# One decoder layer for a prompt and a sample group: second half of the layer with channels on the partitions

## The chip, the cores and the metric

The kernel runs on one core of one Trainium2 chip, in 4-byte floats. The metric is the device time of one execution in microseconds (us). A core has TensorE (PE, matrix products into PSUM), VectorE (DVE), ScalarE (ACT), GpSimd (POOL), and SyncE (SP), whose queue starts the DMAs here.

## The reference, cut to what matters

One layer serves a prompt of 2048 tokens and 8 sample tokens; the width is 1024, the feed-forward's 4096.

```
mix = concatenate([o_r, o_m]) @ w_out                 # o_r, o_m: the two mixers' outputs
h  = layer_norm(ALPHA * x + mix, ln1_g, ln1_b)        # mean and variance over the 1024 channels
ff = square(relu(h @ w_ff1)) @ w_ff2
y  = layer_norm(ALPHA * h + ff, ln2_g, ln2_b)
```

The first half of the layer (input projection, an RWKV-7 and a Mamba-2 mixer, and the states) is the same before and after, and so is what the two norms compute.

## The kernel before

The prompt is cut into 4 blocks of 512 tokens. The sample's 8 tokens ride along with block 1 (`smp` in the code). First comes the input projection of all blocks; the mixers of block 0 run beside it. Then `tail(b)` computes output projection, first norm, feed-forward and second norm of each block, and the mixers of block b+1 are recorded in between, at a set rate. The order of the instructions on each engine is made when the program is built, from the order of recording, priorities and buffers; each engine then works its own queue in that order.

Every large product is done in three parts (`mm3`, L163 to L168): an operand is split into a high and a low part (`split`, L196: ACT makes the high one, DVE or POOL the difference), and high x high, high x low and low x high add up in PSUM. Weights come in pieces of 128 x 512 (`wpiece`, L202).

In `tail` a matrix of tokens by channels is built, with the tokens on the partitions: four tiles `hs` of 128 tokens x 1024 channels. The output projection (L1287 to L1330) goes by halves of 256 tokens: for each quarter of the channels and each tile, 24 products of 256 columns, whose sum is added to ALPHA x (L1308). Bank statistics (`stats`, L1203), a square root by Newton steps (`rsqrt`, L175) on one or two columns and one ACT step per tile (L1221) give the normalised rows. For the feed-forward channels are wanted on the partitions: TensorE transposes 128 x 128 pieces (`tr`, L1340) and ACT applies gain and bias on the way out of PSUM (L1346), then the split follows. The first FIRST = 4 tiles of the feed-forward are done for the first 256 tokens while the second half is still being normalised (L1351), then for the second half (L1363). Gain and bias of the rows themselves, needed for ALPHA h, follow beside the feed-forward (`gain`, L1224). `ff1` (L1440) makes 128 of the 4096 channels for the block, with channels on the partitions. The second matrix (L1392 to L1426) goes by 8 steps g of 4 such tiles: hidden values stationary, 512 channels of the weights moving, 12 products of 512 columns for each of 8 outputs. The sample's 8 hidden columns are split into 16 (`hids`) and have 8 narrow products of 512 columns of their own in each half of a step (L1398 to L1401); its output projection has 16 of 256 columns for each quarter (L1318). `fold16` adds the two parts.

The second norm of block b is recorded during the output projection of block b+1 (`late`, L1314); in the last block it goes tile by tile behind each tile's last addition (`norm`, L1232).

PSUM has three banks of tag b and one of tag a for these products, used in turn (`bank`, L1274).

Of the kernel before, what the change touches and what calls it, by code (L numbers as in the profile page):

```python
# [13 lines left out]
ALU = mybir.AluOpType  # L14
# [9 lines left out]
POOLN = (True, True, False, False)  # L24
# [5 lines left out]
        ("xf", 1), ("uv", 2), ("bt", 1), ("st", 2), ("r1", 1), ("hids", 8))  # L30
# [26 lines left out]
for _name, _w in (  # L57
    ("mu", 14), ("w0", 4), ("a0", 4), ("kk", 4), ("ka", 4), ("rk", 4), ("lnw", 4), ("lnb", 4),
    ("cw", 32), ("cb", 8), ("gn", 4), ("ds", 4), ("g1", 8), ("b1", 8),
# [10 lines left out]
for _name, _w in (  # L70
    ("ident", 128), ("scm", 128), ("m1", 64), ("m2", 64), ("bm", 4), ("d16", 16), ("tri", 128),
    ("b64", 128), ("cen", 128), ("s16", 8), ("sel", 2), ("one", 2),
):
    CCOL[_name] = (_n, _w)
    _n += _w
# [3 lines left out]
def shape_constants():  # L79
# [25 lines left out]
    put("one", 1.0)  # L105
    return c


class K:
# [30 lines left out]
    def wide(self):  # L140
        return self.sb("g4", (128, 2, 520)).rearrange("p a t -> p (a t)")[:, :1024]

# [32 lines left out]
    def rsqrt(self, x, n, p=128):  # L175

        nc = self.nc
        y = self.sm(f"rsy{n}", [128, n])[:p]
        t = self.sm(f"rst{n}", [128, n])[:p]
# [4 lines left out]
        if n == 1:  # L184
            nc.vector.tensor_scalar(out=x, in0=x, scalar1=-0.5, scalar2=None, op0=ALU.mult)
        for _ in range(3):
            if n == 1:
                nc.vector.scalar_tensor_tensor(out=t, in0=y, scalar=x, in1=y, op0=ALU.mult, op1=ALU.mult)
                nc.vector.scalar_tensor_tensor(out=y, in0=t, scalar=1.5, in1=y, op0=ALU.add, op1=ALU.mult)
            else:  # L190
                nc.vector.scalar_tensor_tensor(out=t, in0=y, scalar=-0.5, in1=y, op0=ALU.mult, op1=ALU.mult)
                nc.vector.tensor_mul(t, t, x)
                nc.vector.scalar_tensor_tensor(out=y, in0=t, scalar=1.5, in1=y, op0=ALU.add, op1=ALU.mult)
# [39 lines left out]
    def setup_mix(self):  # L233
# [79 lines left out]
        self.osT = self.mp.tile([128, 8, 16], F32R, name="osT")  # L313
# [25 lines left out]
    def load_o(self, b, half):  # L339
        return self.load_act(lambda k: self.s_o[b][:, k, :], range(4 * half, 4 * half + 4))  # L340
# [594 lines left out]
    def sample(self):  # L935
# [162 lines left out]
        os_ = t(8, 8)  # L1098
# [86 lines left out]
        self.split(os_, self.osT[:, :, 0:8], self.osT[:, :, 8:16])  # L1185
# [17 lines left out]
    def stats(self, h, bs, q):  # L1203
        self.nc.vector.bn_stats(bs[:, q, :], h[:, q * 512:(q + 1) * 512])

    def ln(self, tiles, bs, p):

        nc = self.nc
        n = len(tiles)
        mv = self.sm("mv", [128, 4, 2])[:p, :n]  # L1210
        for i in range(n):
# [417 lines left out]
```

## Time and profile before

| | |
|---|---|
| median of 3 runs | 2891.64 us (2886.47 to 2894.46) |
| profiled execution | 2881.87 us |
| its span | 2880.1 us |
| mean granted TensorE clock | 0.982 of full speed |
| PE, DVE, ACT, POOL busy | 97%, 69%, 45%, 13% |

The profile is of one execution. Busy times are shares of the span from the first to the last instruction. Two TensorE products are in flight at a time, so the duration of one is longer than the distance from one start to the next; that distance is the rate. A 4-byte product that is not split (weights and data as plain floats) stands in the trace as two instructions.

### The profile page before, as it was taken

To read this page: it belongs to the slowest core of one execution; us is meant where nothing else is said; L and a number is where in the kernel's file an instruction comes from. 1 tells how busy PE (TensorE), PEld (TensorE's weight loads), DVE (VectorE), ACT (ScalarE), POOL (GpSimd) and SP (SyncE) were. 2 spreads that over 40 slices of the span, in tenths; PEclk is the share of its full clock that TensorE was granted. 3 is DMA by queue.
4 is the path that set the end of the run, shared out by engine and by line. 5 is a ranking of instruction groups with operands and counts; after the bars stand their busy time and mean duration, and the time that the engine had idled before them with its cause. 6 is when DMAs were issued, how large, how long until landed. Compare 5 with 4: busy or idle time off the path is not lost.

```text
span 2880.1 us, 52319 instructions
## 1 busy us (share of the span) xinstructions
PE 2786.3 (97%) x19114; PEld 2310.9 (80%) x19114; DVE 1979.4 (69%) x4841; ACT 1285.9 (45%) x2493; POOL 364.5 (13%) x508
## 2 busy tenths in 40 slices
PE   9999999999989999998899999998999999899997
PEld 7798987777878777787788888887777778888886
DVE  7878878878777767676866666568766656754446
ACT  5554644554536333434544444336343334543332
POOL 2322212222321000002200000022000001200001
PEclk9999999999989999998999999999999999899999
DMA  6655655555744434346434344254443335433232
GB/s 207 191 169 150 185 152 165 156 176 160 211 138 133 131 110 130 110 125 215 136 93 120 115 116 121 85 196 131 120 138 114 109 103 167 158 103 95 88 103 70
DMA packets 333766, 395.54 MB, mean 137 GB/s; under 512 B 84990, under 2 KB 191060, under 8 KB 333500
## 3 DMA queue, kind: packets, MB, share of 16 engines
q1 hardware_dynamic: 333508, 392.20, 45.4%
q8 instruction: 150, 2.46, 0.4%
q14 instruction: 108, 0.88, 0.1%
HBM read 331.32 MB, written 60.81 MB: 136 GB/s over the span
## 4 chain that ended last, share of the span: by engine, by line
PE 79%; DVE 10%; DMA 4%; issue 4%; ACT 2%; SPq 1%; POOL 0%; DVEq 0%; POOLq 0%; ACTq 0%
PE psb L166 18%; PE psb L167 18%; PE psb L168 17%; PE psm L152 7%; PE psa L166 4%; PE psa L168 4%; PE psa L167 4%; PE psc L152 2%; PE psa L152 2%; PE psb L152 1%; DVE w L200 1%; PE psm L173 1%; PE psy L741 1%; DVE lr L655 1%; DVE rX L656 1%
## 5 line engine op out<-in xcount | busy, mean ns | idle before, releaser
L199 ACT ACTIVATE w<-wr 128x512 fp32r<-128x512 f32 (+1 forms) x836 | 518.8, 627 | 604.5 <-PE psb L168 237.2
L200 DVE TENSOR_TENSOR w<-wr,w 128x512 fp32r<-128x512 f32 x712 | 510.8, 722 | 230.3 <-ACT w L199 226.5
L166 PE MATMUL psb<-act,w 128*128 128x512 f32 (+2 forms) x1768 | 628.4, 356 | 6.3 <-ACT act L199 5.5
L167 PE MATMUL psb<-act,w 128*128 128x512 f32 (+2 forms) x1768 | 621.1, 352 | 0.6 <-DVE act L200 0.6
L168 PE MATMUL psb<-act,w 128*128 128x512 f32 (+2 forms) x1768 | 616.9, 349 | 0.0
L166 PEld LDWEIGHTS psb<-act,w 128*128 128x128 f32 x1768 | 335.9, 190 | 55.5 <-ACT act L199 6.0
L168 PEld LDWEIGHTS psb<-act,w 128*128 128x128 f32 x1768 | 336.3, 190 | 45.6 <-DVE w L200 0.2
L167 PEld LDWEIGHTS psb<-act,w 128*128 128x128 f32 x1768 | 337.0, 191 | 44.7 <-DVE act L200 2.6
L166 PE MATMUL psb<-w,g 128*128 128x512 f32 x788 | 317.0, 404 | 9.5 <-ACT w L199 9.5
L167 PE MATMUL psb<-w,g 128*128 128x512 f32 x788 | 314.6, 399 | 0.0
L168 PE MATMUL psb<-w,g 128*128 128x512 f32 x788 | 312.5, 397 | 0.0
L200 POOL TENSOR_TENSOR w<-wr,w 128x512 fp32r<-128x512 f32 x124 | 180.2, 1458 | 717.5 <-ACT w L199 703.6
L1504 DVE TENSOR_TENSOR g<-psb,g 128x512 f32<-128x512 f32 x173 | 118.8, 687 | 163.2 <-PE psb L168 162.6
L166 PEld LDWEIGHTS psb<-w,g 128*128 128x128 f32 x788 | 148.6, 189 | 46.1 <-ACT w L199 10.3
L168 PEld LDWEIGHTS psb<-w,g 128*128 128x128 f32 x788 | 148.4, 188 | 33.6 <-DVE g L200 0.2
L167 PEld LDWEIGHTS psb<-w,g 128*128 128x128 f32 x788 | 149.0, 189 | 32.5 <-DVE w L200 0.2
L200 DVE TENSOR_TENSOR g<-r,g 128x256 fp32r<-128x256 f32 (+1 forms) x172 | 97.1, 565 | 82.5 <-ACT g L199 81.6
L1454 ACT ACTIVATE r<-psb 128x512 f32<-128x512 f32 (+2 forms) x130 | 63.2, 487 | 190.2 <-PE psb L168 188.3
L166 PE MATMUL psa<-act,w 128*128 128x256 f32 (+2 forms) x336 | 116.4, 346 | 0.0
L167 PE MATMUL psa<-act,w 128*128 128x256 f32 (+2 forms) x336 | 114.6, 341 | 0.0
L168 PE MATMUL psa<-act,w 128*128 128x256 f32 (+2 forms) x336 | 114.1, 340 | 0.0
L655 DVE TENSOR_TENSOR lr<-rX,lr 128x4 f32<-128x4 f32 (+14 forms) x480 | 100.7, 210 | 10.8
(389 smaller groups left out, 5207.3 us busy)
## 6 DMA issues: line engine op xcount, KB each, us to landing
wr<-in_w_ff_dram SPq DMA_DIRECT2D x512, 256.0 KB
wr<-in_w_in_dram SPq DMA_DIRECT2D x208, 256.0 KB
wr<-in_w_out_dram SPq DMA_DIRECT2D x112, 256.0 KB
lr<-d_l SPq DMA_DIRECT2D x256, 64.0 KB
s_m<-g SPq DMA_DIRECT2D x48, 256.0 KB
ms<-s_m SPq DMA_DIRECT2D x16, 768.0 KB
wr<-in_xT_dram SPq DMA_DIRECT2D x32, 256.0 KB
s_ar<-g SPq DMA_DIRECT2D x16, 512.0 KB
```

Of the source, the lines that this page charges most:

```text
L152: return self.nc.tensor.matmul(out, l, r, start=start, stop=stop)
L166: nc.tensor.matmul(out, l[0], r[0], start=first, stop=False)
L167: nc.tensor.matmul(out, l[0], r[1], start=False, stop=False)
L168: nc.tensor.matmul(out, l[1], r[0], start=False, stop=last)
L173: self.nc.tensor.transpose(out, in_, self.cst[p0:p0 + k, o + p0:o + p0 + k])
L199: nc.scalar.activation(hi, raw, AF.Copy)
L200: (eng or nc.vector).tensor_tensor(out=lo, in0=raw, in1=hi.bitcast(F32), op=ALU.subtract)
L655: nc.vector.tensor_tensor(out=row, in0=X[:, :, s + 1:16], in1=row, op=ALU.mult)
L656: nc.vector.tensor_reduce(X[:, :, s:s + 1], lr[:, :, 17 * s:16 * s + 16], axis=AX.X, op=ALU.add)
L741: acc = lambda o, l, r, start, stop: nc.tensor.matmul(o, l, r, start=start, stop=stop, skip_group_check=True)
L1454: nc.scalar.activation(rl, ps, AF.Relu)
L1504: self.nc.vector.tensor_tensor(out=h, in0=ps, in1=h, op=ALU.add)
```

## The change

Everything in `tail` now has the channels on the partitions: `hs` are four tiles of 128 x 2 x 520, two groups of 128 channels each, with 512 tokens and the sample's 8 behind them. The weights become the stationary operand of output projection and second matrix, the activations the moving one. ALPHA x is loaded from the transposed input, and the result is stored transposed; the host turns it round. The sample's tokens are 8 more columns of the second half (264 in place of 256); for that the second matrix goes by halves in block 1, and also in the last step of the last block, where the first half's norm is recorded between the second half's products.

A norm is now done for 256 (or 264) tokens at a time, over channels on the partitions. Means come from TensorE: eight products with a column of ones, each giving 32 equal rows, in four column groups of the array, so that four partial sums stand on 4 x 32 partitions; ACT copies them to SBUF, and one 128 x 128 product with a constant adds them and gives every partition the mean. The same is done with the squares. `rsqrt` works on the full 128 x 256. There are no transposes, no bank statistics, no `fold16`, and no gain and bias over rows; gain and bias are ACT's scale and bias again.

The core of the diff:

```diff
+    def chan_mean(self, src, m, held):
+        p = self.bank()
+        one = self.con("one")[:, 0:1].to_broadcast([128, 32])
+        self.row([(p[32 * (k % 4):32 * (k % 4) + 32, :m], one, src(k), k < 4, k >= 4) for k in range(KT)], held)
+        part = self.sb("r", (128, 512))[:, :m]
+        self.nc.scalar.activation(part, p[:, :m], AF.Copy)
+        p = self.bank()[:, :m]
+        self.mm(p, self.con("mean").to_broadcast([128, 128]), part)
+        return p
+
+    def norm(self, hs, o, m, gain, bias, put, held):
         nc = self.nc
+        seg = [h[:, :, o:o + m] for h in hs]
+        wide = lambda a: a.unsqueeze(1).to_broadcast([128, 2, m])
+        mean = self.chan_mean(lambda k: seg[k // 2][:, k % 2, :], m, held[o])
+        yield
+        sqs = []
+        for h in seg:
+            nc.vector.tensor_tensor(out=h, in0=h, in1=wide(mean), op=ALU.subtract)
+            sqs.append(self.sb("sq", (128, 2, 264))[:, :, :m])
+            sq = nc.scalar.activation(sqs[-1], h, AF.Square)
+        yield
+        var = self.chan_mean(lambda k: sqs[k // 2][:, k % 2, :], m, sq)
+        ln = self.sb("ln", (128, 3, 264))
+        x, y, t = (ln[:, i, :m] for i in range(3))
+        nc.vector.tensor_scalar(out=x, in0=var, scalar1=LN_EPS, scalar2=None, op0=ALU.add)
+        rs = self.rsqrt(x, m, yt=(y, t))
+        yield
+        for q, h in enumerate(seg):
+            nc.vector.tensor_tensor(out=h, in0=h, in1=wide(rs), op=ALU.mult)
+            for a in range(2):
+                k = 2 * q + a
+                nc.scalar.activation(h[:, a], h[:, a], AF.Identity, scale=self.par(gain, k), bias=self.par(bias, k))
+            put(q)
             yield
...
+        for half, (o, m) in enumerate(cols):
+            for i in range(KT):
+                k = i if half == 0 else KT - 1 - i
+                if half == 0 or i:
+                    wo = [self.wpiece(A["w_out"][k, :, h * 512:(h + 1) * 512], (4, 128)) for h in range(2)]
...
+                ps = self.bank()[:, :m]
+                for c in range(KT):
+                    l = [wo[c // 4][s][:, c % 4, :] for s in range(2)]
+                    r = [act[c][:, s, o:o + m] for s in range(2)]
+                    self.mm3(ps, l, r, c == 0, c == KT - 1)
+                held[o] = self.accum(hs[k // 2][:, k % 2, o:o + m], ps, True)
+                next(ln, 0)
+                next(self.late, 0)
+                yield 2.6
             for _ in ln:
                 pass
+            ln = self.norm(hs, o, m, "g1", "b1", split_hT(o, m), held)
...
+        norms = [self.norm(hs, o, m, "g2", "b2", store(o, m), held) for o, m in cols]
...
+            end = last and nxt is None
+            for o, m, k in [(o, m, k) for o, m in cols for k in range(KT)] if end else \
+                    [(o, m, k) for k in range(KT) for o, m in segs]:
...
+                ps = self.bank()[:, :m]
                 for f in range(4):
-                    l = [hid[f][0][:, s, i * 128:(i + 1) * 128] for s in range(2)]
-                    r = [w2[f][s][:, 0, :] for s in range(2)]
+                    l = [w2[k // 4][f][s][:, 0, c] for s in range(2)]
+                    r = [hid[f][0][:, s, o:o + m] for s in range(2)]
                     self.mm3(ps, l, r, f == 0, f == 3)
+                held[o] = self.accum(hs[k // 2][:, k % 2, o:o + m], ps, g == 0)
...
+                if end and o:
+                    next(norms[0], 0)
...
+        self.late = itertools.chain(*norms)
```

How the queues change is shown at three places. The first is VectorE's queue in the move from block 2 to block 3, from the last addition of the output projection on. `psb_28160` is the PSUM bank of the last output projection group, `g_...` are tiles of `hs`, `w_` weight pieces being split, `obs` and `omv` statistics, `act_` the operands of the feed-forward. Before:

```order
L1308 SCALAR_TENSOR_TENSOR g_4513_27859<-g_4513_27859,psb_28160 128x256
L200 TENSOR_TENSOR w_28404<-wr_28402,w_28404 128x512
L1204 BN_STATS obs_27446<-g_4513_27859 128x6
L1212 BN_AGGR omv_28298<-obs_27446 128x2
L200 TENSOR_TENSOR act_28193<-r_28197,act_28193 128x256
L200 TENSOR_TENSOR act_28201<-r_28205,act_28201 128x256
```

Now, where `psb_28885` holds the mean of the second norm of block 2 (`g_3496`, `g_3511`), `act_28819` to `act_28871` belong to the first half of block 3, and `ln_` are the square root's tiles; `psb_28897` is the last output projection group:

```order
L1403 SCALAR_TENSOR_TENSOR g_4408_28088<-g_4408_28088,psb_28897 128x256
L1214 TENSOR_TENSOR g_3496_22606<-g_3496_22606,psb_28885 128x2x256
L190 TENSOR_TENSOR act_28819<-g_4442_28312,act_28819 128x256
L190 TENSOR_TENSOR act_28822<-g_4442_28312,act_28822 128x256
L1214 TENSOR_TENSOR g_3511_22736<-g_3511_22736,psb_28885 128x2x256
L190 TENSOR_TENSOR act_28868<-g_4455_28414,act_28868 128x256
L190 TENSOR_TENSOR act_28871<-g_4455_28414,act_28871 128x256
L190 TENSOR_TENSOR w_29153<-wr_29151,w_29153 128x512
L1221 TENSOR_SCALAR ln_28948<-psb_28946 128x256
```

Behind the last addition there now stands the rest of the norm of the block before, and then, from the 21st instruction on, the block's own second half; the first operand of that half is the 48th instruction behind the addition.

The second place is TensorE's queue at the same point. Before, transposes (L173) follow the last output projection group, and `psb_28194`, `psb_28202` are their banks:

```order
L168 MATMUL psb_28160<-w_28127,act_27392 128x256
L173 MATMUL psb_28194<-cst,g_4462_27467 128x128
L173 MATMUL psb_28194<-cst,g_4463_27469 128x128
L173 MATMUL psb_28202<-cst,g_4462_27467 128x128
L173 MATMUL psb_28202<-cst,g_4463_27469 128x128
```

Now the sums of squares (`sq_`) of the block before follow, then the spreading product (`r_28944` is the copy of its partial sums), and the feed-forward (`psb_28988`):

```order
L165 MATMUL psb_28897<-act_28027,w_28894 128x256
L149 MATMUL psa_28935<-sq_28924,cst 32x256 x2
L149 MATMUL psa_28935<-sq_28927,cst 32x256 x2
L149 MATMUL psa_28935<-sq_28930,cst 32x256 x2
L149 MATMUL psa_28935<-sq_28933,cst 32x256 x2
L149 MATMUL psb_28946<-r_28944,cst 128x256
L163 MATMUL psb_28988<-act_28721,w_28979 128x256
```

No transpose is left, and the sums stand in the queue ahead of products that do not need them.

The third place is the end of TensorE's queue. Before, it ends with the last product of the second matrix:

```order
L166 MATMUL psb_31087<-w_30917,g_5000_30812 128x512
L167 MATMUL psb_31087<-w_30917,g_5000_30812 128x512
L168 MATMUL psb_31087<-w_30917,g_5000_30812 128x512
L1620 UNCONDITIONAL_BRANCH
```

Now mean and variance of the second half of the last block follow it (`g_4408` to `g_4455` are the four tiles, `sq_` their squares):

```order
L165 MATMUL psb_31890<-g_4947_31521,w_31666 128x256
L149 MATMUL psb_31904<-g_4408_28088,cst 32x256 x2
L149 MATMUL psb_31904<-g_4421_28190,cst 32x256 x2
L149 MATMUL psb_31904<-g_4442_28312,cst 32x256 x2
L149 MATMUL psb_31904<-g_4455_28414,cst 32x256 x2
L149 MATMUL psb_31915<-r_31913,cst 128x256
L149 MATMUL psa_31929<-sq_31918,cst 32x256 x2
L149 MATMUL psa_31929<-sq_31921,cst 32x256 x2
L149 MATMUL psa_31929<-sq_31924,cst 32x256 x2
L149 MATMUL psa_31929<-sq_31927,cst 32x256 x2
L149 MATMUL psb_31940<-r_31938,cst 128x256
```

Eighteen 4-byte products, eight for each sum and one to spread it, now stand behind the last large product, where none stood.

## Rows read from the trace of the kernel before

**Rows 1.** The page, part 1: busy us (share of the span) and instructions.
```profile
PE 2786.3 (97%) x19114; PEld 2310.9 (80%) x19114; DVE 1979.4 (69%) x4841; ACT 1285.9 (45%) x2493; POOL 364.5 (13%) x508
```

**Rows 2.** Windows: stretch, us, busy of PE, PEld, DVE, ACT, POOL; clock, DMA, GB/s.
```profile
820.00:900.00 80.00, 69.97 (x662) 62.96 (x661) 55.51 (x146) 45.58 (x102) 17.41 (x16) 0.86 0.51 156
1390.00:1450.00 60.00, 50.44 (x396) 41.13 (x394) 45.55 (x127) 33.12 (x75) 10.36 (x10) 0.83 0.42 129
1950.00:1990.00 40.00, 31.59 (x218) 26.62 (x217) 35.72 (x70) 23.31 (x40) 12.81 (x8) 0.87 0.51 165
2480.00:2530.00 50.00, 40.58 (x286) 37.72 (x285) 34.48 (x61) 31.48 (x71) 9.38 (x6) 0.83 0.37 126
2600.00:2800.00 200.00, 200.00 (x864) 161.87 (x862) 86.15 (x128) 74.03 (x124) 0.00 (x0) 1.00 0.31 96
```

**Rows 3.** Waits of TensorE: who waited for whom, us in total, times, longest.
```profile
PE psb L173 <- DVE g L1308: 9.9, 4, 4.7
PE psa L173 <- DVE g L1308: 5.0, 2, 2.9
PE psb L173 <- ACT r L1346: 2.5, 3, 1.3
```

**Rows 4.** Timeline of TensorE in block 1's second matrix: start, duration, operation.
```profile
1914.63 1.32 PE L152 MATMUL psa<-w,hids 128*16 128x512 f32 x5
1915.79 0.39 PE L166 MATMUL psb<-w,g 128*128 128x512 f32 x1
...
1918.58 0.28 PE L166 MATMUL psb<-w,act 128*128 128x256 f32 x1
...
1921.40 0.39 PE L166 MATMUL psb<-w,g 128*128 128x512 f32 x1
```

**Rows 5.** Groups of instructions by shape, TensorE: count, busy us, mean ns, idle before.
```profile
L173 PE MATMUL psb<-cst,g 128*128 128x128 f32 x96 | 22.0, 332 | 12.8 <-DVE g L1308 9.9 <-ACT r L1346 2.5 <-ACT r L1454 0.4
L152 PE MATMUL psb<-w,hids 128*16 128x512 f32 x80 | 21.0, 399 | 0.0
L152 PE MATMUL psb<-w,osT 128*16 128x256 f32 x48 | 6.0, 277 | 0.0
```

**Rows 6.** Timeline of TensorE: mixer products of 64 and of 128 outputs.
```profile
908.48 0.45 PE L152 MATMUL psm<-m,m 128*64 128x128 f32 x4
...
910.43 0.50 PE L166 MATMUL psb<-act,w 128*128 128x512 f32 x1
...
913.79 1.02 PE L152 MATMUL psm<-m,m 128*128 128x256 f32 x4
914.46 0.58 PE L168 MATMUL psb<-act,w 128*128 128x512 f32 x1
```

**Rows 7.** Groups of instructions by shape, VectorE.
```profile
L1504 DVE TENSOR_TENSOR g<-psb,g 128x512 f32<-128x512 f32 x173 | 118.8, 687 | 163.2 <-PE psb L168 162.6
L1226 DVE TENSOR_TENSOR g<-g,g 128x1024 f32<-128x1024 f32 x28 | 36.5, 1310 | 3.9 <-ACT g L1221 2.9 <-PE psb L173 1.0
L1204 DVE BATCH_NORM_STATS2 fbs<-g 128x6 f32<-128x512 f32 x32 | 22.0, 690 | 0.6
L749 DVE TENSOR_TENSOR st<-psc,st 128x256 f32<-128x256 f32 x32 | 13.5, 423 | 19.0 <-PE psc L152 18.7
L582 DVE TENSOR_SCALAR g<-g 128x512 f32<-128x512 f32 x16 | 9.2, 573 | 3.9 <-ACT g L571 3.6
```

**Rows 8.** Timeline of TensorE behind the waits of the last stretch.
```profile
2500.03 0.41 PE L166 MATMUL psb<-act,w 128*128 128x256 f32 x1
...
2500.67 0.42 PE L166 MATMUL psb<-act,w 128*128 128x256 f32 x1
```

**Rows 9.** Groups of instructions by shape, ScalarE.
```profile
L1346 ACT ACTIVATE r<-psb,prm 128x256 f32<-128x256 f32 x42 | 22.6, 559 | 13.9 <-PE psb L173 11.2 <-DVE act L200 2.4
```

**Rows 10.** Timeline: the last large product and the last step of VectorE.
```profile
2864.98 0.40 PE L168 MATMUL psb<-w,g 128*128 128x512 f32 x1
...
2875.23 1.41 DVE L1247 SCALAR_TENSOR_TENSOR g<-g,frsy,g 128x512 f32<-128x512 f32 x2
```

More of the change, by code (lines that the diff above doesn't have):

```diff
@@ L71 @@
     ("ident", 128), ("scm", 128), ("m1", 64), ("m2", 64), ("bm", 4), ("d16", 16), ("tri", 128),
[L72 removed]
+    ("b64", 128), ("cen", 128), ("s16", 8), ("sel", 2), ("one", 2), ("mean", 1),
 ):
@@ L105, in shape_constants @@
     put("one", 1.0)
+    put("mean", 1.0 / (32 * D))
     return c
@@ L339, in load_o @@
     def load_o(self, b, half):
-        return self.load_act(lambda k: self.s_o[b][:, k, :], range(4 * half, 4 * half + 4))
+        return self.load_act(lambda k: self.s_o[b][:, k, :], range(4 * half, 4 * half + 4),
+                             sample=self.osT if b == self.sblk else None)
     def wpieces(self, j, halves=(0, 1)):
@@ L1357, in tail @@
+        first = []
+        for f in range(FIRST):
+            first.append(self.ff1(f, hT, cols[:1]))
+            next(ln, 0)
+            yield 2.6
+        for _ in ln:
+            pass
         self.pf = "f"
-        g1 = self.affine(1)
-        gain = itertools.chain(*([self.gain(h, 128, *g1) for h in hs[:4]] +
-                                 ([self.gain(hs[4][0:8], 8, *g1)] if smp else [])))
-        segs = [(0, 256), (256, 264)] if smp else [(0, 512)]
+        segs = cols if smp else [(0, TB)]
@@ L1362, in tail @@
         done = {}
         for f in range(FIRST):
-            done[f] = self.ff1(f, hT, [(256, W - 256)], first[f])
-            next(gain, 0)
+            done[f] = self.ff1(f, hT, cols[1:], first[f])
             yield 2.6
@@ L1426, in tail @@
-                yield 2.6
-        def finish():
-            if nxt is not None:
-                yield from self.ln(hs[:4], [bs[:, i] for i in range(4)], 128)
-                for i in range(4):
-                    yield from self.gain(hs[i], 128, *ab, rows[i])
-            if smp:
-                yield from self.ln_s(hs[4])
-                yield from self.gain(hs[4][0:8], 8, *ab, A["y_s"])
-        self.late = finish()
+                held[o] = self.accum(hs[k // 2][:, k % 2, o:o + m], ps, g == 0)
@@ L1438, in tail @@
+                if not smp and not end:
+                    held[256] = held[0]
+                if end and o:
+                    next(norms[0], 0)
+                if last and not end and k >= BESIDE and o + m >= TB:
+                    self.pf = "o"
+                    yield next(nxt)
+                    self.pf = "f"
+                yield 2.6 * m / TB
+        self.late = itertools.chain(*norms)
         self.nxt = nxt
```

248 lines of the change are left out of this document (47 added, 201 removed).

## The prediction

> **What bounds the kernel now.** I read the page first: TensorE (PE) is busy 2786 of the 2880.1 us span, VectorE (DVE) 1979, ScalarE (ACT) 1286 [rows 1]. Then the windows: in a feed-forward stretch PE is busy 200.0 of 200 us at full clock, while in the four stretches where one block's norm and output projection give way to the next block's feed-forward it idles 10.0, 9.6, 8.4 and 9.4 us, 37.4 together, at a mean clock of 0.83 to 0.87, with DVE at 69 to 89% [rows 2]. So outside these stretches what counts is the sum of PE's products, and inside them whether DVE, and the chain through it, keeps up. The list of waits names the waiters there: the transposes wait 14.9 us for the last additions of the output projection and 2.5 us for ACT [rows 3].
>
> **Products that only change their form.** Back to back, a 512-column product takes 0.2325 us (12 in 1915.79 to 1918.58) and a 256-column one 0.1175 us (24 in 1918.58 to 1921.40) [rows 4]. The longer durations of the grouped rows overlap, two products being in flight, and are no price. Turning the output projection round changes neither the number nor the width of its products. In the second matrix of the feed-forward 864 products of 512 columns become 1728 of 256 or 264: the 768 of the block with the sample, and 96 in the last quarter-step of the last block. That is 1728 x 0.1175 - 864 x 0.2325 = 2.2 us, and 8 columns more in 768 + 192 of them, 0.0037 us each, 3.5: together 5.7 us.
>
> **Products removed.** The sample's 128 narrow products in the feed-forward take as long as full ones: five of them fill 1914.63 to 1915.79, 0.232 us each [rows 4, 5], 29.8 us. Its 64 in the output projection (rows of 48 and 16; the larger is shown) run at the 256-column rate: 7.5 us. The 128 + 8 transposes cost between 0.1175 us, the 256-column product, and 0.229 us (22.0 us for 96 [rows 5]); I take 0.16, 22 us (16 to 31). In sum 59 us, and 70 or 53 at the ends.
>
> **Products added.** There are 2 norms x 2 token halves x 4 blocks, with a mean and a variance each: 32 sums over channels. Each is eight 4-byte products with 32 outputs, set in four column groups, and one full product that adds and spreads the four parts. A 4-byte product is two instructions: two full ones with 256 columns take 913.79 to 914.46 and hold the next product 0.19 us longer, 0.86 us for four instructions, 0.215 each [rows 6]. The spreading product thus costs 0.43 us. No row has four column groups. The nearest has two: 32 instructions of 128 columns, which one after another would take 32 x 0.1075 = 3.44 us, take 1.95 us (908.48 to 910.43), an overlap of 1.76 [rows 6]. Bounds for the eight: no overlap 16 x 0.215 = 3.44 us, full overlap of four 0.86 us; two-fold 1.95. I take 1.4, between the measured two groups and full four, and keep 0.86 and 3.44. A sum is then 1.83 us, 32 are 58.6 (41 to 124). A price below nothing is excluded: these are instructions that were not there.
>
> The trace shows 1.76 from two column groups [rows 6]. The Trainium skill, TensorEngine Tiling (Array Packing), Theoretical Speedup, promises up to a factor of 4 for 32 outputs; by that the 32 sums would be 32 x (0.86 + 0.43) = 41 us. By the two-group row they would be 32 x (1.95 + 0.43) = 76 us. No run here shows four groups yet.
>
> PE's products together: 5.7 - 59 + 58.6 = +5 us (-23 to +77).
>
> **VectorE and ScalarE.** A 256-wide DVE step with a PSUM operand takes 0.42 us, a 512-wide one 0.69, a statistics step 0.69, a gain or bias step over 1024 columns 1.31 [rows 7]. A half norm is now 8 wide steps (5.5 us), nine 256-wide ones (3.8) and three scalar steps of some 0.3 (half of the 0.57 at 512 columns [rows 7]): 10.2 us, 16 of them 163. Removed are 64 statistics steps (44 us), 56 steps of 1024 columns (73), and the small ones; the load stays near 69%. But its place changes. Before, gain and bias of the first norm came after the critical stretch, beside 99% busy PE; now all of a norm must be done before its result can be split into the two operands of the feed-forward.
>
> The last such stretch, which has no mixer work, shows it. Behind the last addition of the output projection DVE's queue held a statistics step, its short aggregate and one weight split before the first operand; now 15 steps of 512 columns, 27 of 256 and 6 scalar ones stand before the first operand of the second half: 10.3 + 11.4 + 1.8 = 23.5 us. PE has beside it the first-half products of four feed-forward tiles, 96 x 0.1175 = 11.3 us, and three sums, 5.5: it waits 6.7 us. Before it idled 9.4 us in that stretch [rows 2], so the wait changes its place more than its size. What comes on top is the chain: PE, ACT, PE, DVE, ACT, PE, ACT, PE, DVE, ACT, ACT, DVE, some 14 hand-overs for mean and variance, which I put at 0.1 to 0.3 us each, 1.4 to 4.2 us, an estimate from no single row. I take +4 us for each of the four stretches, 16 in all, and keep -9 (the idle time vanishes) and +15 each.
>
> The clock belongs here. After the waits of the last stretch three products start 0.64 us apart (2500.03, 2500.67), 0.213 each, against 0.1175 at full clock [rows 8]: that is 1.2 in place of 2.4 GHz. Waits of the same size will bring this again, so I leave it as it is. ACT's evictions at the transposes go (0.56 us each [rows 9]); the same scale-and-bias step returns in the norm.
>
> **The end.** The last product starts at 2864.98 and ends 0.40 later; the last DVE step begins at 2875.23 and the span ends at 2880.1 [rows 10]: 14.7 us behind the last product, because only the last 128 tokens were left to normalise with one-element-wide square roots. Now the norm of 256 tokens is left. The last addition stands in the queue behind the first half's norm (some 5 us late); then products 1.4 + 0.43, ACT copy 0.4, four subtractions 2.8 and the last square 0.6, products and copy again 2.2, variance to 1/sqrt 4.7, first multiplication 0.7, eight ACT steps of 0.56, 4.5, the store as before from the last step on (3.5), and 2 us of hand-overs: 28 to 29 us. Its cost is +14 us (+8 to +20, the upper with TensorE's part at half clock).
>
> **Sum.** +5 + 16 + 14 = +35 us. The profiled execution took 2881.9 us, so 2917; the median of the runs, 2891.6, lies 9.8 above that one, and against it I say 2925.
>
> **The rivals.**
> 1. *The waits at the transposes go and nothing takes their place.* For it: 17.4 us of waits have exactly this name [rows 3], and the list of PE's work now offers four tiles and three sums in the meantime. Against it: 23.5 us of DVE against 16.8 of PE, counted above. If the four stretches lost their 37.4 us of idle time [rows 2] the sum were 5 + 14 - 37 = -18 us: 2873, faster. It decides from the point where DVE reaches the first operand of the second half within the 17 us.
> 2. *Column groups do not overlap.* 32 x 2.04 = 65 us more: 2990. Against it stands the 1.76 of two groups.
> 3. *DVE becomes the bound of the four stretches.* With late norms of the block before (21 us of DVE where gains and biases were 11), a PSUM bank stays taken until its four subtractions are through, and PE's few banks run out; at 15 us a stretch in place of 4, and the clock at half behind it: 44 to 60 us more, 2970 to 2985. For it: DVE is at 89% in the third of these stretches already.
> 4. *It cancels:* cheap sums (41 us) and no extra wait: 5 - 18 + 14 = +1 us, 2893.
>
> By the skill's factor of 4 alone, nothing else changed, the time would be 2907.
>
> **How the numbers follow.** Forecast (slower by 15 to 55 us, 2907 to 2947) 0.48; rival 1 0.20; rival 2 0.07; rival 3 0.13; rival 4 0.12. A measurement of this kernel tells about 0.3% (9 us) from no change. Faster: rival 1 and a little of rival 4, 0.22. The same: most of rival 4, 0.12. Slower: 0.66. The range from 2875 to 2985 leaves out the better half of rival 1 and most of rival 2; the forecast's own is 2907 to 2947.
>
> **What would show it.** Right: PE's 32-output products as groups with 1.2 to 1.6 us for eight, no PE wait on transposes, waits of the second-half feed-forward products on the split of 6 to 12 us in each of four stretches, and 26 to 31 us from the last feed-forward product to the end. The sums wrong: eight products taking 0.9 or over 2 us. The stretches wrong: PE idle there below 5 us or above 15. It would all be wrong if the block with the sample ran slower than the other blocks by more than 10 us beyond its sums, since its 12-product groups now last 1.4 us in place of 2.8 and DVE must clear a bank in half the time.

## The result and the profile after

The changed kernel takes 2904.7 us (median of 5; 2899.5 to 2909.1) against 2886.5 us of the kernel before on the same chip: a ratio of 1.0064 (95%: 1.0048 to 1.0080), 14 to 23 us slower. Run again later, on a chip where the kernel before took 2883.5 us, it took 2909.6: 1.0090 (1.0074 to 1.0105), 21 to 30 us. The direction was forecast rightly, the size was not: against the 2925 us of the forecast and its range of 2907 to 2947, the first measurement lies 2 us below the range and the second inside it. The profiled executions lie apart by 2908.95 - 2881.87 = 27.1 us, and so do their spans (2907.2 - 2880.1). That difference can be followed through the program.

TensorE's products cost next to nothing more. The first row of the page [rows 1] now reads, for PE and PEld, DVE, ACT and POOL:

```profile
PE 2789.2 (96%) x20218; PEld 2354.5 (81%) x20218; DVE 1973.7 (68%) x4815; ACT 1310.5 (45%) x2582; POOL 348.4 (12%) x504
```

PE is busy 2.9 us longer, so that 24.2 of the 27.1 us are time in which it waits. The windows with the same clock times as before [rows 2] show that the waits are still in the stretches between two blocks, and none in the feed-forward of the last block, from 2600 to 2800 us (two of the four stretches, and that one; columns as in rows 2):

```profile
1390.00:1450.00 60.00, 46.43 (x422) 39.12 (x422) 53.92 (x118) 39.87 (x92) 9.39 (x8) 0.88 0.38 117
2480.00:2530.00 50.00, 33.54 (x261) 26.84 (x261) 41.33 (x83) 31.68 (x71) 7.13 (x5) 0.87 0.31 101
2600.00:2800.00 200.00, 200.00 (x865) 162.12 (x864) 85.63 (x127) 73.67 (x124) 0.00 (x0) 1.00 0.29 94
```

Fixed windows catch other work after than before. It is better to cut both traces at the same event of the program. I take the ends of ScalarE's evictions of feed-forward tiles: in each block the twelfth (both halves of the first four tiles are through, and four more) and the last (in block 0 the last but four, ahead of the sample's final steps). First the kernel before, then the changed one: up to block 0's feed-forward; the change from block 0 to 1; block 1's feed-forward (with the sample); the changes from 1 to 2 and from 2 to 3; the end.

```profile
0.00:962.91 962.91, 929.89 (x6559) 775.05 (x6560) 745.30 (x1857) 479.67 (x914) 218.68 (x368) 0.99 0.58 168
1259.87:1471.86 211.99, 193.07 (x1300) 167.13 (x1300) 160.83 (x364) 103.03 (x207) 34.49 (x28) 0.91 0.52 163
1471.86:1887.90 416.04, 414.71 (x3444) 352.55 (x3440) 256.48 (x698) 175.80 (x405) 15.75 (x24) 1.00 0.37 109
1887.90:2074.82 186.92, 174.01 (x1266) 146.96 (x1264) 146.57 (x337) 90.25 (x174) 34.47 (x28) 0.97 0.49 157
2419.83:2576.20 156.37, 146.91 (x903) 130.73 (x902) 105.22 (x190) 78.32 (x146) 28.79 (x18) 0.95 0.49 163
2843.42:2880.10 36.68, 21.96 (x94) 17.06 (x92) 28.83 (x74) 4.71 (x7) 10.95 (x8) 0.85 0.15 58
```

```profile
0.00:964.36 964.36, 929.26 (x6599) 772.83 (x6600) 750.95 (x1885) 480.25 (x924) 219.57 (x369) 0.99 0.56 167
1264.55:1473.03 208.48, 188.66 (x1334) 162.12 (x1334) 157.00 (x348) 111.09 (x239) 32.65 (x29) 0.93 0.50 154
1473.03:1873.92 400.89, 395.89 (x4005) 382.09 (x4001) 248.39 (x716) 162.56 (x365) 15.39 (x24) 1.00 0.37 113
1873.92:2071.65 197.73, 179.19 (x1456) 155.18 (x1452) 146.24 (x326) 98.82 (x204) 33.01 (x29) 0.95 0.45 141
2416.20:2588.72 172.52, 155.97 (x1015) 133.46 (x1014) 108.01 (x192) 88.82 (x179) 26.44 (x19) 0.95 0.42 139
2855.64:2907.20 51.56, 33.12 (x259) 25.92 (x257) 26.70 (x58) 16.04 (x31) 0.00 (x0) 0.83 0.12 41
```

From row to row: +1.5, -3.5, -15.2, +10.8, +16.2 and +14.9 us; the feed-forwards in between add 2.5. The idle time of PE (length less busy time) grows in the four changes of block (the first is the way into block 0's feed-forward) by 2.1, 0.9, 5.6 and 7.1, 15.7 us together, at the end by 3.7, and in the feed-forwards of blocks 0 to 2, where it waits at the mixers' products, by 4.8.

The waits have other names. Those at the transposes [rows 3] are gone with the transposes; the list of PE's waits now begins:

```profile
PE psa L149 <- ACT sq L1216: 26.0, 6, 8.8
PE psb L163 <- ACT act L189: 13.9, 6, 5.4
PE psm L149 <- DVE xs L651: 9.9, 5, 7.0
```

The first is the products that sum the squares of a late norm (the block before's second norm, which is not urgent), the second the feed-forward's wait for split operands, which the prediction had as the main one. The timeline of all engines at the last change of block shows the first:

```profile
2493.22 0.28 PE L165 MATMUL psb<-act,w 128*128 128x256 f32 x1
...
2494.47 2.50 DVE L1225 TENSOR_TENSOR g<-g,ln 128x512 f32<-128x512 f32 x4
...
2497.56 1.28 DVE L1214 TENSOR_TENSOR g<-g,psb 128x512 f32<-128x512 f32 x2
...
2501.59 2.18 ACT L1216 ACTIVATE sq<-g 128x512 f32<-128x512 f32 x4
...
2502.26 2.63 PE L149 MATMUL psa<-sq,cst 128*32 128x256 f32 x16 [8.77 <-ACT sq L1216]
```

PE ends the output projection at 2493.5. What was left of the late norm has been issued in one piece at that place, ahead of the feed-forward, so PE's queue stands on its squares. ScalarE comes to them at 2501.59, behind eight scale-and-bias steps and eight splits of the urgent norm, and VectorE subtracts the late mean only from 2497.56, behind the multiplications of the urgent one. Such waits of 6.4, 6.2 and 8.8 us stand in the last three changes of block. On the way into block 0's feed-forward, where there is no late norm yet, no such wait stands.

The sums themselves, in a dense place and as groups of the whole run (count, busy us, mean ns, idle before; rows 5 and 6 are what they replace or were priced from):

```profile
2487.49 1.07 PE L149 MATMUL psb<-g,cst 128*32 128x256 f32 x16
2488.49 0.55 PE L170 MATMUL psm<-cst,hst 128*128 128x128 f32 x3
```

```profile
L149 PE MATMUL psb<-g,cst 128*32 128x256 f32 x224 | 15.6, 385 | 1.4 <-DVE g L1404 1.4
L149 PE MATMUL psa<-sq,cst 128*32 128x256 f32 x96 | 12.3, 540 | 19.8 <-ACT sq L1216 19.8
```

Eight products, 16 instructions, take 1.00 us from 2487.49 to 2488.49, against 16 x 0.215 = 3.44 one after another: an overlap of 3.4. Over the whole run (starts to starts, waits left out) it is 1.43 us, because products of squares come at the pace in which ScalarE makes them: sums of means take 1.05 us on average, sums of squares 1.8. The Trainium skill, TensorEngine Tiling (Array Packing), Theoretical Speedup, gives a factor of up to 4 for 32 outputs; the 3.4 of the dense place is near it.

The end, behind the last feed-forward product [rows 10], as a window and as VectorE's timeline:

```profile
2882.30:2907.20 24.90, 6.50 (x37) 2.08 (x36) 12.28 (x25) 11.15 (x22) 0.00 (x0) 0.64 0.24 85
```

```profile
2884.35 0.42 DVE L1404 TENSOR_TENSOR g<-psb,g 128x256 f32<-128x256 f32 x1
2888.28 2.48 DVE L1214 TENSOR_TENSOR g<-g,psb 128x512 f32<-128x512 f32 x4 [3.52 <-PE psb L149]
2893.89 0.42 DVE L1221 TENSOR_SCALAR ln<-psb 128x256 f32<-128x256 f32 x1 [3.12 <-PE psb L149]
...
2899.20 2.50 DVE L1225 TENSOR_TENSOR g<-g,ln 128x512 f32<-128x512 f32 x4
```

Last addition, mean, subtraction, variance, eleven steps to its inverse root (2894.35 to 2899.1), multiplication: VectorE has nothing else left to do beside this chain.

### The profile page after: what moved, and what is told of

It is laid out like the page before. It is cut to its first block, busy times and chain, and to the rows that moved or that the text cites. A ratio compares the mean times of both kernels' runs of the same rounds, so it can differ in the third digit from the quotient of the medians.

```text
span 2907.2 us, 54654 instructions
## 1 busy us (share of the span) xinstructions
PE 2789.2 (96%) x20218; PEld 2354.5 (81%) x20218; DVE 1973.7 (68%) x4815; ACT 1310.5 (45%) x2582; POOL 348.4 (12%) x504
## 4 chain that ended last, share of the span: by engine, by line
PE 78%; DVE 10%; DMA 5%; ACT 3%; issue 3%; SPq 1%; POOL 0%; DVEq 0%; ACTq 0%; POOLq 0%
PE psb L163 18%; PE psb L164 17%; PE psb L165 17%; PE psm L149 6%; PE psa L163 4%; PE psa L164 4%; PE psa L165 4%; PE psc L149 2%; PE psa L149 2%; DVE w L190 1%; PE psb L149 1%; PE psm L170 1%; PE psy L732 1%; DVE lr L646 1%; ACT g L1228 1%
## 5 line engine op out<-in xcount | busy, mean ns | idle before, releaser
L163 PE MATMUL psb<-act,w 128*128 128x512 f32 (+2 forms) x2152 | 744.7, 347 | 15.7 <-ACT act L189 13.9
L164 PE MATMUL psb<-act,w 128*128 128x512 f32 (+2 forms) x2152 | 734.5, 342 | 0.9 <-DVE act L190 0.9
L165 PE MATMUL psb<-act,w 128*128 128x512 f32 (+2 forms) x2152 | 729.7, 339 | 0.9 <-POOL w L190 0.9
L190 DVE TENSOR_TENSOR w<-wr,w 128x512 fp32r<-128x512 f32 x716 | 503.9, 709 | 259.1 <-ACT w L189 252.0
L163 PEld LDWEIGHTS psb<-act,w 128*128 128x128 f32 x2152 | 412.0, 192 | 70.3 <-ACT act L189 15.3
L163 PE MATMUL psb<-g,w 128*128 128x512 f32 (+2 forms) x1316 | 457.6, 348 | 3.7 <-ACT w L189 2.0
L164 PE MATMUL psb<-g,w 128*128 128x512 f32 (+2 forms) x1316 | 451.6, 343 | 0.0
L165 PEld LDWEIGHTS psb<-act,w 128*128 128x128 f32 x2152 | 411.8, 191 | 47.5 <-POOL w L190 1.1
L165 PE MATMUL psb<-g,w 128*128 128x512 f32 (+2 forms) x1316 | 449.4, 342 | 0.2 <-DVE w L190 0.2
L164 PEld LDWEIGHTS psb<-act,w 128*128 128x128 f32 x2152 | 412.7, 192 | 45.4 <-DVE act L190 2.2
L163 PEld LDWEIGHTS psb<-g,w 128*128 128x128 f32 x1316 | 248.0, 189 | 37.3 <-ACT w L189 2.9
L165 PEld LDWEIGHTS psb<-g,w 128*128 128x128 f32 x1316 | 248.4, 189 | 30.3 <-DVE w L190 1.1
L164 PEld LDWEIGHTS psb<-g,w 128*128 128x128 f32 x1316 | 248.4, 189 | 27.9 <-issue 0.5
L1404 DVE TENSOR_TENSOR g<-psb,g 128x512 f32<-128x512 f32 (+2 forms) x221 | 126.4, 573 | 161.1 <-PE psb L165 160.6
L163 PE MATMUL psa<-act,w 128*128 128x256 f32 (+2 forms) x464 | 152.3, 328 | 2.8 <-DVE ln L1221 1.5
L164 PE MATMUL psa<-act,w 128*128 128x256 f32 (+2 forms) x464 | 150.4, 324 | 0.0
L165 PE MATMUL psa<-act,w 128*128 128x256 f32 (+2 forms) x464 | 149.5, 322 | 0.0
L190 DVE TENSOR_TENSOR g<-r,g 128x512 fp32r<-128x512 f32 (+2 forms) x172 | 95.0, 552 | 77.9 <-ACT g L189 77.0
```

The lines of the kernel that those rows point to most:

```text
L163: nc.tensor.matmul(out, l[0], r[0], start=first, stop=False)
L164: nc.tensor.matmul(out, l[0], r[1], start=False, stop=False)
L165: nc.tensor.matmul(out, l[1], r[0], start=False, stop=last)
L190: (eng or nc.vector).tensor_tensor(out=lo, in0=raw, in1=hi.bitcast(F32), op=ALU.subtract)
L1404: return self.nc.vector.tensor_tensor(out=h, in0=ps, in1=h, op=ALU.add)
```

## Experiments

All are told as ratio to the kernel before, measured beside them. The changed kernel itself stands at 1.0064 and 1.0090; distances to it are taken from the middle of the two, 1.0077, and do not contain the 7.5 us by which these two differ. The edits are shown in part, and comments in them are added here. Where idle and busy time of PE over a whole run are compared, the changed kernel's are 118.0 and 2789.2 us in its first profile.

**The changed kernel again.**

> The changed kernel once more, unaltered, to see how far a second profiled execution repeats the first. Theory: the waits repeat, since they come from the order of the instructions: TensorE waits for the squares of a late norm near 1407, 1966 and 2493 us with 5 to 9 us each, and every stretch's length is within 3 us of the first profile. Rival: the first profile (2908.95 us, the upper end of its runs) holds chance waits; then one of the three waits is under 3 us here and the profiled execution is near 2900.

Measured: 2909.6 us, 1.0090 (1.0074 to 1.0105); its profiled execution took 2903.1. The waits are the same:

```profile
PE psa L149 <- ACT sq L1216: 25.9, 6, 8.8
PE psb L163 <- ACT act L189: 13.9, 6, 5.4
```

The theory holds: 6.4, 6.2 and 8.8 us come again at the same products, so they follow from the order of the program, and no stretch differs by more than 3.0 us from the first profile. But here the profiled execution is 6.5 us below the median, in the first set 4.2 above it, and before the change 9.8 below the median that the prediction started from. One profiled execution does not tell where the median lies; these three missed it by 4 to 10 us, on both sides.

**Late norm's steps moved.**

```
-        for _ in self.late: pass            # ahead of the first feed-forward products
         for f in range(FIRST):
             first.append(self.ff1(f, hT, cols[:1]))
             next(ln, 0)
+            next(self.late, 0)              # and one behind each second half tile, the rest after them
```

> What is left of a block's late norm at the end of the next block's output projection is no longer issued in one piece ahead of the first feed-forward products; its steps are issued one by one behind each of the eight half tiles of that feed-forward. Nothing is removed. Theory A (the place in TensorE's in-order queue makes the wait): the waits of 6.4, 6.2 and 8.8 us for the squares of the late norm go, 2 to 4 us of each come back as a wait for the first half's split operands, which ScalarE gives from 2496.6 to 2501.7 in the last stretch while TensorE ran dry at 2493.5; the time falls by 8 to 14 us, to 2891 to 2897. Rival B (VectorE's total work in the stretch makes it): the wait reappears at the products of the second half; the time stays within 4 us of 2904.7.

Measured: 2901.1 us, 1.0055 (1.0041 to 1.0068), 3 to 10 us below the changed kernel (8 us below its second measurement, on the same chip): between the two. Its list of waits (two of its rows) tells why:

```profile
PE psb L163 <- ACT act L189: 16.1, 5, 7.5
PE psa L163 <- ACT act L189: 10.8, 3, 4.6
```

The waits for squares fall from 28.2 us (26.0 and 2.2, by PSUM buffer) to 5.1, and those for the split operands rise from 13.9 to 26.9. The squares' place in PE's queue made the wait, but over half of it (13 of 23 us) comes back as another: the operands of the feed-forward are not ready either. PE's idle time over the whole run falls by 12.0 us, its busy time grows by 6.1; where these 6 us come from is open.

**One refinement of the inverse root.**

```
-        for _ in range(3):
+        for _ in range(1 if yt else 3):     # yt: the wide form, in a norm
```

> The inverse square root of the variance is refined once in place of three times (less exact); six of its eleven steps of 256 columns on VectorE go in each of 16 half norms, 6 x 0.43 = 2.6 us each, 41 us of VectorE's time in all. Theory A (TensorE waits only where its queue stands on a late norm, and at the end): 2.6 us less in each of three such waits and 4 us less at the end, 10 to 13 us in all, 2892 to 2895. Rival B (VectorE's work bounds the stretches, four half norms in each): up to 10 us a stretch and the end besides, 25 to 40 us in all, 2865 to 2880. Rival C (all of this is hidden except at the end): 3 to 4 us, 2901.

Measured: 2878.5 us, 0.9975 (0.9964 to 0.9987): 26 to 33 us below the changed kernel, and faster than before. This is the size of rival B; whether VectorE's work or the length of the chain makes it, the next run tells. Six of the 20 VectorE steps in a half norm (splits not counted) are worth more than the whole change lost, and all of it is idle time of PE: 29.3 us less, while its busy time grows by 0.7.

**The six steps put back, out of the chain.**

```
             put(q)
+            if q == 3:
+                for _ in range(6):
+                    nc.vector.scalar_tensor_tensor(out=t, in0=y, scalar=-0.5, in1=y, op0=ALU.mult, op1=ALU.mult)
```

> One refinement in place of three, as in the run that gave 31 us, but the six steps of 256 columns that fall away are put back as steps without use (their result goes nowhere) behind the last multiplication of each half norm. VectorE has all the work of the changed kernel; only the chain from the variance to its result is 2.6 us shorter. Theory A (the length of the chain decides): most of the gain stays, 18 to 31 us less than the changed kernel, 2875 to 2890. Rival B (VectorE's work in the stretch decides): the gain goes, 2900 to 2910. If it is half and half, 2888 to 2897.

Measured: 2886.5 us, 1.0008 (0.9996 to 1.0020): 16 to 24 us below the changed kernel. About two thirds of the gain stay with all the work in place, so most of it is the length of the chain; the last third is VectorE's work. (The mean granted clock of the runs is 0.986 with six steps fewer and 0.987 here, against 0.981 in the changed kernel; how much of the common gain comes by the clock is not parted.) The windows of the change from block 2 to 3 and of the end part the two; first with six steps fewer, then with them put back (changed kernel: 172.52 and 51.56):

```profile
2400.89:2565.84 164.95, 157.65 (x1015) 135.23 (x1014) 98.22 (x168) 88.77 (x179) 26.82 (x19) 0.96 0.44 144
2832.76:2878.61 45.85, 32.67 (x259) 25.91 (x257) 21.88 (x46) 16.17 (x31) 0.00 (x0) 0.84 0.14 47
```

```profile
2404.64:2576.52 171.88, 160.03 (x1015) 137.55 (x1014) 107.74 (x192) 89.11 (x179) 26.48 (x19) 0.94 0.41 139
2843.44:2889.39 45.95, 32.77 (x259) 25.87 (x257) 26.62 (x58) 16.18 (x32) 0.00 (x0) 0.84 0.14 47
```

At the end it is the chain alone (45.9 both times); in this change of block it is VectorE's work (back to 171.9). The other two changes lie between: from block 0 to 1 208.5 us in the changed kernel, 200.7 with six steps fewer, 204.3 with them put back; from 1 to 2 197.7, 194.0 and 195.1. VectorE's queue shows how the work counts in the change from block 2 to 3:

```profile
2468.02 1.79 DVE L1232 SCALAR_TENSOR_TENSOR ln<-ln 128x256 f32<-128x256 f32 x4
...
2470.06 0.88 DVE L1232 SCALAR_TENSOR_TENSOR ln<-ln 128x256 f32<-128x256 f32 x2
2470.97 0.42 DVE L1221 TENSOR_SCALAR ln<-psa 128x256 f32<-128x256 f32 x1
```

The six spare steps (L1232) of one half norm stand ahead of the first step on the next one's variance (L1221), so they are out of their own chain but in the next one.

**No sums.**

```
-        self.row([(p[32 * (k % 4):32 * (k % 4) + 32, :m], one, src(k), k < 4, k >= 4) for k in range(KT)], held)
-        self.nc.scalar.activation(part, p[:, :m], AF.Copy)
-        self.mm(p, self.con("mean").to_broadcast([128, 128]), part)
+        self.row([(p, self.con("mean").to_broadcast([128, 128]), src(lastk))], held)
```

> The eight 32-output products of every sum over channels and the copy of their parts are left out; the spreading product reads the last of the eight pieces in their place (the means and variances are then not those of the reference). Theory A (the sums stand on TensorE's path with their full price): 32 x 1.43 us by their spacing in the profile, 46, and one copy with its hand-overs, some 0.6 us, in each of the two chains at the end: 46 to 50 us less, 2855 to 2859. Rival B (in the stretches TensorE waits in any case, so that the sums fill idle time there): about half, 20 to 30 us less, 2875 to 2885. Rival C (a sum also holds up what stands behind it): over 60 us less, below 2845.

Measured: 2870.1 us, 0.9948 (0.9935 to 0.9962): 33 to 41 us below the changed kernel, between A and B. In the last change of block the waits are long again, with other names:

```profile
PE psb L163 <- ACT act L189: 8.7, 1, 8.7
PE psa L163 <- ACT act L189: 7.1, 1, 7.1
```

In the profiled execution PE is busy 40.0 us less and idles 6.3 us more, at a mean granted clock of 0.978 over the runs (0.981 with the sums). The sums are worth more than the 18 to 26 us that the change loses, yet they are not all on the path. Every chain is shorter here too, by the products and the copy, so this run does not part product time from chain length.

**The kernel before with fewer transposes.**

```
-                for i in range(2):
+                for i in range(1 if one else 2):     # one: not the half with the sample
```

> The kernel before with 56 of its 128 transposes of 128 columns left out; ScalarE reads the one that is left twice, so that its work and VectorE's stay (half of the tokens of these tiles get the wrong values). In the profile of before these transposes follow each other at 0.204 us each (26.1 us for 128), waits left out. Theory A (they stood on TensorE's path): 56 x 0.204 = 11 us less than before, a ratio near 0.996. Rival B (the stretch is bound by VectorE and ScalarE, and TensorE's transposes filled time in which it would have waited): 0 to 4 us less, 0.9985 to 1.000. Rival C (they also held up what VectorE does next): 15 us or more less, below 0.995.

Measured: 2891.7 us, 1.0025 (1.0013 to 1.0036): no gain. Rival B, with a small loss that none of the theories has. The change from block 2 to 3 (before: 156.37, PE busy 146.91):

```profile
2428.26:2585.24 156.98, 144.92 (x887) 128.97 (x886) 105.96 (x190) 78.03 (x145) 28.49 (x18) 0.95 0.49 161
```

PE has 2.0 us less to do there and waits 2.6 us longer. Over the whole run PE idles 105.1 us where it idled 93.8, 11.3 more, about what these transposes took, and its busy time falls by 2.2 only. So leaving out these transposes had no worth in the kernel before: they filled a wait that VectorE and ScalarE set. Nearly 3 us of the loss of 4 to 10 show at the change from block 0 to 1, the rest in no one place. The loss goes with a lower granted clock: six of the seven runs have 0.977 to 0.979 where the kernel before has 0.982 on average, and the one with 0.982 took 2885.8 us. That the longer waits bring the lower clock is likely, but not shown.

**The sum of squares in one pass.**

```
+        nc.scalar.activation(self.meanr, self.con("mean").to_broadcast([128, 128]), AF.Copy, scale=32.0)
-        var = self.chan_mean(lambda k: sqs[k // 2][:, k % 2, :], m, sq)
+        var = self.bank()[:, :m]
+        self.row([(var, self.meanr, sqs[k // 2][:, k % 2, :], k == 0, k == KT - 1) for k in range(KT)], sq)
```

> The sum of the squares becomes eight one-pass fp32r products with all 128 outputs of 1/1024 (ScalarE writes the squares as fp32r); the 32-output products, the copy of the parts and the spreading product go for the 16 variances, and stay for the 16 means. TensorE: 16 x (1.43 + 0.42 - 8 x 0.1175) = 14.6 us less; the chain to each variance loses the copy (0.38 us), the spreading product and two hand-overs, some 1.0 us. Theory A (the sums count on TensorE's path with 39/46 of their time, as the run without sums showed): 12 us there and 1 at the end, near 13 less than the changed kernel. Rival B (what decides is how late VectorE gets the variance; a chain shorter by 1 us counts in each of the stretches besides): 16 to 22 us less. Rival C (hidden behind VectorE's own work): 0 to 6 us less.

Measured: 2884.7 us, 1.0004 (0.9993 to 1.0014): 17 to 25 us below the changed kernel, as fast as before. Rival B. Leaving out less TensorE time than the run without sums, it gains over half as much. PE's busy time falls by 5.8 us only, its idle time by 14.3 (both profiled executions lie 4.2 us above their medians): what counts is that the variance comes earlier, through one step instead of three.

**The last tokens in three pieces.**

```
+        ends = [(0, 256), (256, 128), (384, 128)] if b == self.nb - 1 else cols
-            for o, m, k in [(o, m, k) for o, m in cols for k in range(KT)] if end else \
+            for o, m, k in [(o, m, k) for o, m in ends for k in range(KT)] if end else \
```

> The last quarter of the last block's second matrix and its norm go in three pieces of 256, 128 and 128 tokens in place of two of 256. Behind the last product are now the steps of 128 columns. Theory A (the end is the chain of VectorE and ScalarE behind the last product, 24.9 us in the profile, and its steps shrink with their columns): subtractions, eleven steps, multiplications and ScalarE's eight steps, 2.5 + 5.1 + 2.5 + 3.9 of those 24.9 us, take some 60% of that, and TensorE's two sums half: 24.9 becomes 17 to 19, the 192 products of 128 columns in place of 96 of 256 may cost 1 to 3 us more: 4 to 7 us less in all than the changed kernel. Rival B (VectorE's queue, which still holds the norms of the earlier pieces when the last sum is ready, decides): within 2 us of it. Rival C (the narrow products cost more than they give): 3 to 8 us more.

Measured: 2927.9 us, 1.0153 (1.0137 to 1.0169): 18 to 26 us above the changed kernel. Rival C's sign, at three to four times its size. Two places of PE's timeline:

```profile
2870.18 0.27 PE L163 MATMUL psb<-g,w 128*128 128x128 f32 x1
2870.29 0.28 PE L164 MATMUL psb<-g,w 128*128 128x128 f32 x1
...
2888.16 0.41 PE L163 MATMUL psb<-g,w 128*128 128x128 f32 x1
2888.38 0.41 PE L164 MATMUL psb<-g,w 128*128 128x128 f32 x1
```

A product of 128 columns is spaced 0.111 us, where one of 256 is spaced 0.1175: half the columns, nearly the same time. The products of the first piece of 128 tokens thus take nearly as long as those of 256 did. Then PE waits 1.4 and 2.4 us at the next norm's mean, the granted clock falls, and most of the last piece runs in this window:

```profile
2884.20:2908.50 24.30, 21.82 (x121) 20.04 (x120) 10.23 (x32) 7.74 (x19) 0.00 (x0) 0.52 0.13 45
```

At a granted clock of 0.52, nearly all of it at 1.2 GHz, the spacing is 0.213. Some 80 of the last piece's 96 products run so: the two pieces cost 112 x 0.111 + 80 x 0.213 = 29.5 us where 96 x 0.1175 = 11.3 did the same before, 18 us more. Theory A is right in its other half: behind the last product now lie 18.2 us in place of 24.8. These 6.6 us are lost again, 3.7 of them to the two waits; the rest fits the sums of a third norm, which stand in PE's queue now.

**Both shortenings.**

```
-        for _ in range(3):
+        for _ in range(2 if yt else 3):
(and the one-pass sum of squares)
```

> The one-pass sum of squares, and the inverse square root refined twice in place of three times (VectorE: 16 x 3 x 0.43 = 21 us less). If the two act on different bounds (TensorE's products and VectorE's chain) the gains add: half of the 31 us that two refinements fewer gave, 15, and 13 from the sums: 28 less than the changed kernel, 2877 to 2882. If the one only uncovers the other: the larger of the two, 13 to 16 less, 2889 to 2892. If each frees the other: over 34 less, below 2872.

Measured: 2871.1 us, 0.9959 (0.9945 to 0.9973): 30 to 38 us below the changed kernel. They add, at least, if two refinements alone are worth half of what one is worth; no run has them alone. With an inverse root refined twice this is faster than both kernels.

**With these, the late norm moved: wholly behind the urgent one, or as above.**

```
                 next(ln, 0)
+                if half == 0:
                     next(self.late, 0)
```

> The one-pass sum of squares and two refinements (2871 us), and besides no step of the late norm is issued during the second half of the next output projection; all of it but the first step follows between the half tiles of the next feed-forward, one behind each of the first four, two behind each of the next four. Theory A (the late norm's steps hold up the norm that the feed-forward waits for, on all three engines' queues): 3 stretches with some 3 to 5 us less each, 2856 to 2862. Rival B (they only change places with what waits, as at the last stretch of the run that moved them in part): within 4 us of 2871. Rival C (VectorE and ScalarE then lack the time for the first feed-forward tiles, which stand behind the late norm's steps): over 2876.

> The one-pass sum of squares and two refinements (2871 us), and what is left of the late norm at the end of the output projection is issued one step behind each of the eight half tiles of the feed-forward, as in the run that gave 8 us without them. Theory A (this gain is a third one, of TensorE's queue alone): 5 to 9 us less, 2862 to 2866. Rival B (with the shorter chains the wait for the late norm's squares is mostly gone already): within 4 us of 2871.

Measured: 2870.6 us, 0.9950 (0.9939 to 0.9962), and 2872.8 us, 0.9952 (0.9940 to 0.9964): not to be told from 0.9959. Rival B both times. In the first of them PE still waits 6.8 us at the last change of block:

```profile
PE psb L163 <- ACT act L189: 6.8, 1, 6.8
```

So once the chains are shorter, these two moves of the late norm no longer matter; what is left there is the wait for the urgent norm's second half.

## Why the prediction was right and wrong

The forecast was 2925 us, 33 above the 2891.6 it started from; measured are 2904.7, 18 above the 2886.5 beside it, and 26 the second time. Three steps failed: the waits were put in the wrong place, the end was counted too large, and 9.8 us from profile to median were added that are not the kernel's. On the profiled execution the sum was +35; the trace has 27.1. Step by step:

- *PE's products, +5.* Busy time rose by 2.9. Within it: sums 1.43 and 0.42 us where 1.4 and 0.43 were taken. In block 1's feed-forward 672 wide products and 112 narrow ones (188.0 us from start to start) became 1344 of 256 and 264 columns (169.0). A narrow one was worth 0.243 (0.232 taken); but the new form costs 8 us for these 1344, where 4 were taken, since 0.1258 and not 0.1175 us lie between starts. (In the prediction's bounds the upper end of what is removed adds up to 68 us, not 70.)
- *Waits in the four changes of block, +16.* They are 15.7 (14.2 in the second profiled execution), so the size came out right, but by luck. The place was wrong: three of the largest are at the late norm's squares, which the prediction did not see, and the second half's split waits 0.7, 1.3, 0.8 and 5.4 us, where 6 to 12 us were expected in each stretch. The spread was wrong too: 4 in each were taken, 0.9 to 7.1 came. What was overlooked is that the late norm's steps, which had no part on TensorE before, now stand in TensorE's queue ahead of urgent products.
- *The end, +14.* This term was mis-sized: idle time there grew by 3.7 us. Behind the last product lie 24.9 us, where 28 to 29 were counted (the last addition came 2 us late, not 5), so 10.2 more than before; and of these 6.5 are PE's sums, which the term for 32 sums had already. They were counted twice: 1.83 us for each of two sums in the prediction's figures.
- *Nothing for the mixers' places in the feed-forward.* There PE idles 4.8 us more, for which the prediction has no term.
- *From the profile to the median, +9.8.* That was no property of the kernel: the changed kernel's profiled execution lay 4.2 us above its median, and its second one 6.5 below. Of the 20 us between 2925 and 2904.7, 8 are the sum and 14 this step, less 2 that were rounded off in the forecast.

As to rival 1 (the idle time goes): 33 to 41 us is what leaving out the sums gave, and without them the change would have been faster than before by its interval, 0.9948. It did not come about, because the norm's chain took the place of the transposes' wait. Rival 2 (no overlap of column groups) is out by the 3.4-fold overlap, rival 4 (sums at 41 us, 0.86 us for eight products, and no extra wait) by the 1.43 us measured and by the waits. Rival 3, VectorE as the bound of these stretches, got 0.13 and holds a part of the truth: the six refinement steps, 41 us of VectorE's time, are worth 26 to 33, but mostly as links of the chain and only by a third as load. That the sum of products and waits came out near right hides this: removed transposes were booked at 22 us, and the experiment on the kernel before shows that removing 56 of them gave nothing.

## What to carry to other kernels

In a stretch where TensorE waits, price the chain that ends the wait, step by step, before the products: eight one-pass products in place of a sum, a copy and a second product, and three wide steps fewer on VectorE, were worth 30 to 38 us, and 56 transposes fewer nothing. When an unhurried piece of work gets products of its own, see what stands behind them in TensorE's queue. And take one profiled execution for the differences between stretches only, not for the median.

## What was not expected of the hardware

- fp32r products (4-byte operands in one pass, as the split parts are multiplied) with 128 outputs take 0.111 us for 128 columns, 0.1175 for 256 and 0.2325 for 512 at full clock: 128 columns in place of 256 save next to nothing. In the window from 2870 to 2880 us of the run in three pieces the weight load is busy 9.07 of 10 us. The Trainium skill, TensorE: Matmul & The Clock Gate, LDWEIGHTS (loading the stationary operand), counts a load by its columns over 1.2, by which a load of 128 is estimated at 107 ns; the trace's spacing of 0.111 us at full clock is near it, that of 0.213 us at half clock is twice as long. That loads, not columns, set the pace there fits these numbers, but no run changes the load alone.
- Four column groups of 4-byte products overlap 3.4-fold (1.00 us for 16 instructions), where two groups gave 1.76 [rows 6].
